# Output projection: its matmuls in four forms, two column blocks each

## The chip, the core and the metric

The kernel runs on one core of a Trainium2 chip. The core has five engines that run side by side: TensorE (PE in the profile; its weight loads are listed apart as PEld), VectorE (DVE), ScalarE (ACT), GpSimd (POOL) and SyncE (SP), whose queue issues the transfers here. TensorE writes its results to PSUM, the other operands lie in SBUF. The metric is the device time of one execution in microseconds (us), from runs of the compiled kernel; lower is better.

## The reference

One layer of a hybrid encoder for 256 tokens with 4096 channels, all float32. The part that the change touches is the projection that brings both branches back into the residual stream:

```python
xn = rms_norm(x, norm_in_g)
proj = xn @ w_in                       # 4096 -> 7 * 2048: q, k, v, z_a, a_c, g_c, z_c
y_a = rms_norm(chunked_attention(q, k, v, rel_table), attn_out_g) * silu(z_a)   # 2048 channels
y_c = rms_norm(conv_module(a_c, g_c, ...), conv_out_g) * silu(z_c)              # 2048 channels
h = x + concatenate([y_a, y_c], axis=-1) @ w_out                                # 4096 x 4096
gate = sigmoid(rms_norm(h, ple_norm_g) @ w_ple_gate + b_ple_gate)
h = h + gate * (p @ w_ple)
return rms_norm(h, final_g)
```

## The kernel before

All large products go through one function, `product`. It makes 512 columns of output for all 256 tokens. Tokens lie on PSUM's partitions, so the two halves of 128 tokens have one accumulator each, `acc[0]` and `acc[1]`, of 128 x 512 float32, which is one PSUM bank. The left operand is kept transposed (channels on partitions) and split into two float32r parts, `xh` and `xl`, whose sum is exact; a `big_t` tile holds four blocks of 128 channels, each with both parts for 256 tokens. The weights are split in the same way: `weight_parts` loads 256 rows by 512 columns (512 KB) on SyncE's queue, ScalarE casts them to the high part `wh` (line 147), VectorE subtracts to get the low part `wl` (line 148). Loaded tiles have five buffers, `wh` and `wl` three each.

`accumulate` adds one block of 128 channels for one half of the tokens in three passes: `xh` times `wh` (line 158), `xh` times `wl` (line 159), `xl` times `wh` (line 160). The activations are the stationary operand, 128 x 128, and the weights move, 512 columns at a time. In `product` the loops are: chunks of two channel blocks, then the block, then the token half, then the three passes. A product over 4096 channels is 16 chunks, or 192 matmuls.

The output projection is a loop over eight blocks of 512 output columns. Each loads its part of `x` (tile `hc`), calls `product` on `w_out`, adds the accumulators to `hc` one token half after the other (line 556, VectorE), sums squares (ScalarE), and transposes the result with eight TensorE transposes of 128 x 128 (line 118) into the operand of the gate product, which is split on ScalarE and VectorE (lines 106 and 107).

No order is written by hand around this loop. The tile framework schedules the instructions and puts in the semaphores; it moves the eight transposes of a block behind the first matmuls of the next one, so that the residual adds have time to finish. Accumulators have four buffers in PSUM, which is two products' worth. After the projection come the embedding products over two channel blocks, whose stationary tile is `pT_in`, and the gate products.

Of the kernel before, what the change touches and what calls it, by code (L numbers as in the profile page):

```python
# [16 lines left out]
P = 128  # L17
NB = 512
# [6 lines left out]
def hybrid_block(  # L25
# [23 lines left out]
    nc = tc.nc  # L49
    _, T, D = x.shape  # L50
    NH = T // P
# [3 lines left out]
    HD = AW // H  # L55
# [3 lines left out]
    KD = D // P  # L59
    KCW = CW // P  # L60
    GH = NB // HD
# [21 lines left out]
    nc.gpsimd.memset(mhalf, -0.5)  # L83

    def rsqrt(dst, src, n):
        """dst = (src / n + eps) ** -0.5, element by element."""
        nc.vector.tensor_scalar(dst, src, 1.0 / n, EPS, ALU.mult, ALU.add)  # L87
        nc.gpsimd.tensor_tensor(dst, dst, mhalf[:, : dst.shape[1]], ALU.pow)  # L88

# [1 line left out]
    gin_rows = cpool.tile([KD, P], F32, name="gin_rows")  # L91
    nc.sync.dma_start(gin_rows, norm_in_g[0].rearrange("(k q) -> k q", q=P))
    gin_ps = tmp_psum()
# [2 lines left out]
    with tc.high_priority():  # L96
        nc.vector.tensor_copy(g_in, gin_ps[:, :KD])

# [1 line left out]
    def big_tile():  # L100
        return big.tile([P, 4, 2, T], F32R, tag="big", name="big_t")

    def split_from_psum(dst, i, src, scale):
        """dst[:, i] = the exact float32r parts of src * scale, a [128, T] block."""
        hi, lo = dst[:, i, 0, :], dst[:, i, 1, :]
        nc.scalar.activation(hi, src, AF.Identity, scale=scale)  # L106
        nc.vector.scalar_tensor_tensor(  # L107
            lo, src, scale, hi.bitcast(F32), ALU.mult, ALU.subtract
        )

    def transposed_split(src, dst, g, col0):
        """src [128, NH, 512] (tokens in rows) to dst's four blocks of [128, T]."""
        for pair in range(2):
            pt = tmp_psum()
            for i in range(2):
                b = 2 * pair + i
                for h in range(NH):
                    nc.tensor.transpose(  # L118
                        pt[:, i * T + h * P : i * T + (h + 1) * P],
                        src[:, h, b * P : (b + 1) * P],  # L120
                        ident,
                    )
            for i in range(2):
                b = 2 * pair + i
                split_from_psum(dst, b, pt[:, i * T : (i + 1) * T], g[:, col0 + b : col0 + b + 1])

# [1 line left out]
    later = deque()  # L128

    def fill(n):  # L130
        for _ in range(min(n, len(later))):
            later.popleft()()

# [1 line left out]
    def weight_parts(w, col, k0, kc, tiles=None):  # L135
        """Rows of kc blocks from block k0: the float32r parts of w, high and low."""
        wt = wpool.tile([P, KC, NB], F32, tag="w", name="wt")
        nc.sync.dma_start(
            wt[:, :kc, :],
            w[k0 * P : (k0 + kc) * P, col : col + NB].rearrange("(k q) n -> q k n", q=P),  # L140
        )
        if tiles is None:
            tiles = [
                wpool.tile([P, KC, NB], F32R, tag=tag, name=tag, bufs=3) for tag in ("wh", "wl")
            ]
        wh, wl = tiles
        nc.scalar.copy(wh[:, :kc, :], wt[:, :kc, :])  # L147
        nc.vector.tensor_tensor(  # L148
            wl[:, :kc, :], wt[:, :kc, :], wh[:, :kc, :].bitcast(F32), ALU.subtract
        )  # L150
        return wh, wl

    def accumulate(acc, h, lhs, kb, wh, wl, k, kblocks):
        t, i = lhs[kb // 4], kb % 4
        xh = t[:, i, 0, h * P : (h + 1) * P]
        xl = t[:, i, 1, h * P : (h + 1) * P]
        first, last = kb == 0, kb == kblocks - 1
        nc.tensor.matmul(acc, xh, wh[:, k, :], start=first, stop=False)  # L158
        nc.tensor.matmul(acc, xh, wl[:, k, :], start=False, stop=False)  # L159
        nc.tensor.matmul(acc, xl, wh[:, k, :], start=False, stop=last)  # L160

    def product(w, col, lhs, kblocks, pool=None, tag="acc", ahead=None, lag=()):
        """[tokens, 512] in PSUM, one tile for each half of the tokens. With lag, pairs of
        tiles that keep the last weights, the second half stops before those and comes with
        a function that adds them."""
        acc = [
            (pool or ps_acc).tile([P, NB], F32, tag=tag, name=f"acc{h}") for h in range(NH)
        ]
        starts = list(range(0, kblocks, KC))
        kept = starts[len(starts) - len(lag) :] if lag else []  # L170
        held = []
        for k0 in starts:
            kc = min(KC, kblocks - k0)
            keep = k0 in kept
            wh, wl = weight_parts(w, col, k0, kc, lag[kept.index(k0)] if keep else None)
            if keep:
                held.append((k0, kc, wh, wl))
            for k in range(kc):
                for h in range(1 if keep else NH):
                    accumulate(acc[h], h, lhs, k0 + k, wh, wl, k, kblocks)  # L180
            if ahead:
                ahead(k0 + kc)
            fill(2)

        def rest():
            for k0, kc, wh, wl in held:
                for k in range(kc):
                    accumulate(acc[1], 1, lhs, k0 + k, wh, wl, k, kblocks)

        return (acc, rest) if lag else acc  # L190
# [8 lines left out]
        rsqrt(r, r, n)  # L199
        return r  # L200

# [1 line left out]
    ssq_x = cpool.tile([P, NH, D // NB], F32, name="ssq_x")  # L203
    xT = []

# [12 lines left out]
        )  # L218

    def load_ahead(kb):  # L220
        """Called after the products of the blocks before kb; the next four are half done."""
        if kb % 4 == 2 and kb // 4 + 1 < D // NB:
            load_x(kb // 4 + 1)

# [35 lines left out]
            dw[:, 4 * c : 4 * c + 4, :], dps[:, : 4 * 32].rearrange("q (i t) -> q i t", t=32)  # L260
        )

# [1 line left out]
    conv = []  # L264

    def conv_tap(cv, uT, i, b, k):
# [38 lines left out]
                later.append(partial(conv_tap, cv, uT, i, 4 * c + i, k))  # L305
        conv.append(cv)

# [1 line left out]
    uS = []  # L309

    def layer_norm_swish():
        """Adds the steps to the work that waits; they leave the split result in uS."""
        add = nc.gpsimd.tensor_tensor
        st = {}

# [10 lines left out]
            nc.scalar.copy(st[key], m)  # L326

        def mean(s):
            """Mean over all channels, on every partition."""
            m = tmp_psum()  # L330
            nc.tensor.matmul(m[:, :T], mean_w, fold(s), start=True, stop=True)
            stat("mu", m[:, :T])
# [18 lines left out]
                add(st["q"], st["q"], s, ALU.add)  # L351

        def variance(s):
            """1 / deviation of each token, tokens on partitions."""
            s = fold(s)
            m = tmp_psum()
            for h in range(NH):
                nc.tensor.matmul(
                    m[:, h : h + 1], s[:, h * P : (h + 1) * P], mean_w[:, :1],
                    start=True, stop=True,  # L360
                )
            st["r"] = cpool.tile([P, NH], F32, name="r_ln")
            rsqrt(st["r"], m[:, :NH], 1)

        def spread(s):
            """The same on every partition, tokens along the free axis."""
            m = tmp_psum()
            for h in range(NH):
                d = s[:, 0, h * P : (h + 1) * P]
# [33 lines left out]
        for c in range(n):  # L403
            later.extend(partial(split, c, i) for i in range(4))

# [1 line left out]
    y_a = []  # L407
    ssq_a = cpool.tile([P, NH, AW // NB], F32, name="ssq_a")

    def to_heads(acc, name):  # L410
        """[tokens, GH * HD] times 1 / rms to [HD, GH, tokens]."""
        st = spool.tile([P, NH, NB], F32, tag="stage", name="st")
        for h in range(NH):
            nc.scalar.activation(st[:, h, :], acc[h], AF.Identity, scale=r_x[:, h : h + 1])
# [83 lines left out]
        heads(g)  # L498
    r_a = rstd_of(ssq_a, AW, "r_a")

# [1 line left out]
    def broadcast_row(src, n0, n):  # L502
        """src[n0 : n0 + n] on every partition."""
        t = spool.tile([P, n], F32, tag="row", name="row")
        nc.sync.dma_start(
            t, bass.AP(tensor=src.tensor, offset=src.offset + n0, ap=[[0, P], [1, n]])
        )
        return t
# [11 lines left out]
        y_c.append(y)  # L520
    r_c = rstd_of(ssq_c, CW, "r_c")

# [1 line left out]
    def gated(y, col, r_y):  # L524
        acc = product(w_in0, col, xT, KD)
        sz = spool.tile([P, NH, NB], F32, tag="stage", name="sz")
# [16 lines left out]
    for c, y in enumerate(y_c):  # L543
        to_operand(y, gc, c)

# [1 line left out]
    hs, hT = [], []  # L547
    ssq_h = cpool.tile([P, NH, D // NB], F32, name="ssq_h")
    for c in range(D // NB):
# [1 line left out]
        nc.sync.dma_start(  # L551
            hc, x[0, :, c * NB : (c + 1) * NB].rearrange("(h q) n -> q h n", q=P)
        )
        acc = product(w_out[0], c * NB, yT, KD)
        for h in range(NH):
            nc.vector.tensor_tensor(hc[:, h, :], acc[h], hc[:, h, :], ALU.add)
            square_sum(ssq_h[:, h, c : c + 1], hc[:, h, :])
# [3 lines left out]
        hT.append(t)  # L561
    r_h = rstd_of(ssq_h, D, "r_h")

# [1 line left out]
    pin = spool.tile([P, NH, PLE], F32, tag="stage", name="pin")  # L565
    nc.sync.dma_start(pin, p[0, 0].rearrange("(h q) n -> q h n", q=P))
    pT = spool.tile([P, PLE // P, 2, T], F32R, tag="hd", name="pT_in", bufs=5)
# [5 lines left out]
            )  # L573
        split_from_psum(pT, b, ppt[:, b * T : (b + 1) * T], 1.0)

# [1 line left out]
    n_f = D // NB  # L577
    ssq_f = cpool.tile([P, NH, n_f], F32, name="ssq_f")

# [75 lines left out]
```

## Time and profile before

| | us |
|---|---|
| median of 3 runs | 2128.86 |
| lowest and highest run | 2128.04, 2129.68 |
| span of the profiled execution, first to last instruction | 2126.7 |
| TensorE busy in it | 2100.4 |
| weight loads busy | 1730.7 |
| VectorE busy | 1268.0 |
| ScalarE busy | 963.2 |

The profile has one execution. Its own time is shown as the span; what lies around the span is in the runs alone. Matmuls overlap in the pipeline: the duration of one is longer than the distance from its start to the next one's start, so the busy times of the three passes add up to more than the span. The output projection runs from about 1384 to 1742 us of the span. In the chain of waits a row gives the start, the length and the work that held the end up; in the timeline a row gives start, length, engine, line and operands, and equal neighbours are merged with their count.

### The profile page before, as it was taken

How to read it: one execution, taken by the hardware profiler on the slowest of the kernel's cores; microseconds unless marked ns; L12 is line 12 of the kernel's file. 1: busy time of each engine (PE TensorE's matmuls, PEld its weight loads, DVE VectorE, ACT ScalarE, POOL GpSimd, SP SyncE). 2: the span in 40 equal slices, each digit the busy share in tenths (PEclk: the TensorE clock that was granted, in tenths of full speed). 3: DMA queues.
4: the chain of work that ended last, by engine and by line, in shares of the span. 5: the costliest groups of instructions: out<-in, count | busy, mean ns of one | idle time of the engine just before them, and what ended most of it. 6: DMA issues, size and time to landing. Idle time of an engine off the chain costs nothing.

```text
span 2126.7 us, 25003 instructions
## 1 busy us (share of the span) xinstructions
PE 2100.4 (99%) x9456; PEld 1730.7 (81%) x9456; DVE 1268.0 (60%) x1609; ACT 963.2 (45%) x1195; POOL 76.3 (4%) x66
## 2 busy tenths in 40 slices
PE   8999999999999999999999999999999999999997
PEld 6788888888888888888888888888888888888886
DVE  5499975498547946765455544464454455455554
ACT  6344445444444444654444444454444454444444
POOL 0000000000000002200000000000000001111110
PEclk9999999999999999999999999999999999999999
DMA  8566665666666665555666666665666656666664
GB/s 273 174 189 192 188 189 177 195 189 187 179 190 188 189 199 167 179 177 198 200 202 203 199 196 191 198 219 188 189 190 192 191 179 206 200 205 201 206 203 173
DMA packets 215065, 412.23 MB, mean 194 GB/s; under 512 B 12948, under 2 KB 15908, under 8 KB 214944
## 3 DMA queue, kind: packets, MB, share of 16 engines
q1 hardware_dynamic: 214944, 410.63, 62.4%
q8 instruction: 74, 1.21, 0.2%
q14 instruction: 47, 0.39, 0.1%
HBM read 406.39 MB, written 4.19 MB: 193 GB/s over the span
## 4 chain that ended last, share of the span: by engine, by line
PE 97%; issue 1%; DMA 1%; DVE 1%; ACT 0%; POOL 0%; SPq 0%; ACTq 0%; POOLq 0%; DVEq 0%
PE acc L158 31%; PE acc L159 31%; PE acc L160 31%; PE tmp_ps L118 1%; PE tmp_ps L421 0%; DMA dwr<-in_w_dw_dram 0%; PE tmp_ps L436 0%; PE tmp_ps L454 0%; DVE cv L343 0%; DMA wt<-in_w_in_dram 0%; DVE wl L148 0%; PE tmp_ps L294 0%; PE tmp_ps L460 0%; PE tmp_ps L461 0%; PE tmp_ps L435 0%
## 5 line engine op out<-in xcount | busy, mean ns | idle before, releaser
L148 DVE TENSOR_TENSOR wl<-wt,wh 128x1024 fp32r<-128x1024 f32 x740 | 919.4, 1244 | 777.4 <-ACT wh L147 776.3
L147 ACT CAST wh<-wt 128x1024 fp32r<-128x1024 f32 x740 | 779.2, 1053 | 1050.5 <-PE acc L160 983.5
L158 PE MATMUL acc<-wh,big_t 128*128 128x512 f32 x2928 | 1146.2, 391 | 5.6 <-ACT big_t L106 5.6
L159 PE MATMUL acc<-wl,big_t 128*128 128x512 f32 x2928 | 1146.6, 392 | 0.6 <-DVE wl L148 0.6
L160 PE MATMUL acc<-wh,big_t 128*128 128x512 f32 x2928 | 1144.1, 391 | 0.0
L158 PEld LDWEIGHTS acc<-wh,big_t 128*128 128x128 f32 x2928 | 550.7, 188 | 119.0 <-ACT big_t L106 6.0
L159 PEld LDWEIGHTS acc<-wl,big_t 128*128 128x128 f32 x2928 | 551.4, 188 | 113.1 <-DVE wl L148 1.3
L160 PEld LDWEIGHTS acc<-wh,big_t 128*128 128x128 f32 x2928 | 551.1, 188 | 113.1
L272 DVE SCALAR_TENSOR_TENSOR cv<-uT,dw,cv 128x256 f32<-128x256 f32 x480 | 201.5, 476 | 0.5
L586 POOL TENSOR_TENSOR hc<-hc,gt 128x512 f32<-128x512 f32 x14 | 24.7, 1784 | 289.8 <-PE acc L160 160.7
L106 ACT ACTIVATE big_t<-tmp_ps,prm 128x256 fp32r<-128x256 f32 x64 | 27.1, 474 | 11.4 <-PE acc L160 5.9
L107 DVE SCALAR_TENSOR_TENSOR big_t<-tmp_ps,prm,big_t 128x256 fp32r<-128x256 f32 x64 | 27.9, 478 | 6.5 <-ACT big_t L106 6.0
L194 ACT ACTIVATE junk<-hc 128x512 bf16<-128x512 f32 x32 | 20.0, 625 | 16.9 <-POOL hc L586 13.9
L88 POOL TENSOR_TENSOR r_h<-r_h,mhalf 128x2 f32<-128x2 f32 x1 | 0.7, 692 | 710.7 <-DVE r_h L87 710.7
L447 ACT ACTIVATE s<-s,nm 128x128 f32<-128x128 f32 (+1 forms) x32 | 14.3, 447 | 9.5 <-DVE nm L446 9.5
L589 POOL TENSOR_TENSOR hc<-hc,row 128x512 f32<-128x512 f32 x14 | 17.8, 1292 | 0.0
L582 DVE SCALAR_TENSOR_TENSOR gt<-acc,r_h,row 128x512 f32<-128x512 f32 x16 | 11.3, 745 | 10.1 <-PE acc L160 10.1
L463 ACT ACTIVATE y_a<-tmp_ps,den 128x128 f32<-128x128 f32 x32 | 10.0, 363 | 14.2 <-PE tmp_ps L461 14.2
L107 DVE SCALAR_TENSOR_TENSOR big_t<-tmp_ps,g_in,big_t 128x256 fp32r<-128x256 f32 x32 | 14.1, 478 | 3.7 <-ACT big_t L106 3.7
L106 ACT ACTIVATE big_t<-tmp_ps,g_in 128x256 fp32r<-128x256 f32 x32 | 13.7, 470 | 5.2 <-DVE big_t L107 3.8
L442 DVE SCALAR_TENSOR_TENSOR s<-tmp_ps,bias 128x128 f32<-128x128 f32 (+1 forms) x32 | 9.9, 352 | 8.9 <-PE tmp_ps L436 8.9
L583 ACT ACTIVATE gt<-gt 128x512 f32<-128x512 f32 x16 | 9.3, 624 | 12.3 <-DVE gt L582 12.3
(136 smaller groups left out, 511.7 us busy)
## 6 DMA issues: line engine op xcount, KB each, us to landing
wt<-in_w_in_dram SPq DMA_DIRECT2D x448, 512.0 KB, 3.7
wt<-in_w_out_dram SPq DMA_DIRECT2D x128, 512.0 KB, 3.5
wt<-in_w_ple_gate_dram SPq DMA_DIRECT2D x128, 512.0 KB, 4.3
wt<-in_w_pw_dram SPq DMA_DIRECT2D x32, 512.0 KB, 3.8
hc<-in_x_dram SPq DMA_DIRECT2D x8, 512.0 KB, 4.2
wt<-in_w_ple_dram SPq DMA_DIRECT2D x8, 512.0 KB, 4.3
out_dram<-hc SPq DMA_DIRECT2D x16, 256.0 KB, 2.8
xin<-in_x_dram SPq DMA_DIRECT2D x7, 512.0 KB, 7.2
```

Source lines behind the costliest of these rows:

```text
L106: nc.scalar.activation(hi, src, AF.Identity, scale=scale)
L107: nc.vector.scalar_tensor_tensor(lo, src, scale, hi.bitcast(F32), ALU.mult, ALU.subtract)
L118: nc.tensor.transpose(pt[:, i * T + h * P : i * T + (h + 1) * P], src[:, h, b * P : (b + 1) * P], ident,)
L147: nc.scalar.copy(wh[:, :kc, :], wt[:, :kc, :])
L148: nc.vector.tensor_tensor(wl[:, :kc, :], wt[:, :kc, :], wh[:, :kc, :].bitcast(F32), ALU.subtract)
L158: nc.tensor.matmul(acc, xh, wh[:, k, :], start=first, stop=False)
L159: nc.tensor.matmul(acc, xh, wl[:, k, :], start=False, stop=False)
L160: nc.tensor.matmul(acc, xl, wh[:, k, :], start=False, stop=last)
L194: nc.scalar.activation(junk, src, AF.Square, accum_out=dst)
L272: nc.vector.scalar_tensor_tensor(cv[:, i, :], uT[:, i, k : k + T], dw[:, b, k : k + 1], cv[:, i, :], ALU.mult, ALU.add,)
L586: (nc.vector if last else nc.gpsimd).tensor_tensor(hc, hc, gt, ALU.add)
L589: nc.gpsimd.tensor_tensor(hc, hc, fg, ALU.mult)
```

## The change

The eight column blocks of the output projection take four forms, two blocks each. Blocks 0 and 1 stay as they were. Blocks 2 and 3 ("turns") put the token halves in turns inside each pass: all three passes alternate between `acc[0]` and `acc[1]`. Blocks 4 and 5 ("narrow") cut every matmul into two of 256 columns, with the same stationary block, one after the other. Blocks 6 and 7 ("moving") exchange the second and third pass, so that `wh` moves twice in a row and `wl` comes last. Every product is the same sum of the same three terms; all other products of the kernel keep the old form.

```diff
+    def parts(h, lhs, kb):
+        t, i = lhs[kb // 4], kb % 4
+        return tuple(t[:, i, j, h * P : (h + 1) * P] for j in range(2))
+
     def accumulate(acc, h, lhs, kb, wh, wl, k, kblocks):
-        t, i = lhs[kb // 4], kb % 4
-        xh = t[:, i, 0, h * P : (h + 1) * P]
-        xl = t[:, i, 1, h * P : (h + 1) * P]
+        xh, xl = parts(h, lhs, kb)
...
+    def accumulate_turns(acc, lhs, kb, wh, wl, k, kblocks):
+        first, last = kb == 0, kb == kblocks - 1
+        for j, (part, w) in enumerate(((0, wh), (0, wl), (1, wh))):
+            for h in range(NH):
+                nc.tensor.matmul(
+                    acc[h], parts(h, lhs, kb)[part], w[:, k, :],
+                    start=first and j == 0, stop=last and j == 2,
+                )
+
+    def accumulate_narrow(acc, h, lhs, kb, wh, wl, k, kblocks):
+        xh, xl = parts(h, lhs, kb)
+        first, last = kb == 0, kb == kblocks - 1
+        for j, (xp, w) in enumerate(((xh, wh), (xh, wl), (xl, wh))):
+            for n in range(2):
+                cols = slice(n * NB // 2, (n + 1) * NB // 2)
+                nc.tensor.matmul(
+                    acc[:, cols], xp, w[:, k, cols],
+                    start=first and j == 0 and n == 0, stop=last and j == 2,
+                    skip_group_check=True,
+                )
+
+    def accumulate_moving(acc, h, lhs, kb, wh, wl, k, kblocks):
+        xh, xl = parts(h, lhs, kb)
+        first, last = kb == 0, kb == kblocks - 1
+        nc.tensor.matmul(acc, xh, wh[:, k, :], start=first, stop=False)
+        nc.tensor.matmul(acc, xl, wh[:, k, :], start=False, stop=False)
+        nc.tensor.matmul(acc, xh, wl[:, k, :], start=False, stop=last)
...
-    def product(w, col, lhs, kblocks, pool=None, tag="acc", ahead=None, lag=()):
+    def product(w, col, lhs, kblocks, pool=None, tag="acc", ahead=None, lag=(), form=None):
...
             for k in range(kc):
+                if form == "turns":
+                    accumulate_turns(acc, lhs, k0 + k, wh, wl, k, kblocks)
+                    continue
+                one = {"narrow": accumulate_narrow, "moving": accumulate_moving}.get(form, accumulate)
                 for h in range(1 if keep else NH):
-                    accumulate(acc[h], h, lhs, k0 + k, wh, wl, k, kblocks)
+                    one(acc[h], h, lhs, k0 + k, wh, wl, k, kblocks)
...
-        acc = product(w_out[0], c * NB, yT, KD)
+        acc = product(
+            w_out[0], c * NB, yT, KD, form=(None, "turns", "narrow", "moving")[c // 2]
+        )
```

The rest of the difference only removes comments and docstrings, so line numbers move.

## The prediction

> **What bounds the kernel.** I read the page first: shares of the span, clock, chain, costliest groups.
>
> ```profile
> span 2126.7 us, 25003 instructions
> PE 2100.4 (99%) x9456; PEld 1730.7 (81%) x9456; DVE 1268.0 (60%) x1609; ACT 963.2 (45%) x1195; POOL 76.3 (4%) x66
> PEclk9999999999999999999999999999999999999999
> PE 97%; issue 1%; DMA 1%; DVE 1%; ACT 0%; POOL 0%; SPq 0%; ACTq 0%; POOLq 0%; DVEq 0%
> PE acc L158 31%; PE acc L159 31%; PE acc L160 31%; PE tmp_ps L118 1%; PE tmp_ps L421 0%; DMA dwr<-in_w_dw_dram 0%; PE tmp_ps L436 0%; PE tmp_ps L454 0%; DVE cv L343 0%; DMA wt<-in_w_in_dram 0%; DVE wl L148 0%; PE tmp_ps L294 0%; PE tmp_ps L460 0%; PE tmp_ps L461 0%; PE tmp_ps L435 0%
> L158 PE MATMUL acc<-wh,big_t 128*128 128x512 f32 x2928 | 1146.2, 391 | 5.6 <-ACT big_t L106 5.6
> L159 PE MATMUL acc<-wl,big_t 128*128 128x512 f32 x2928 | 1146.6, 392 | 0.6 <-DVE wl L148 0.6
> L158 PEld LDWEIGHTS acc<-wh,big_t 128*128 128x128 f32 x2928 | 550.7, 188 | 119.0 <-ACT big_t L106 6.0
> L159 PEld LDWEIGHTS acc<-wl,big_t 128*128 128x128 f32 x2928 | 551.4, 188 | 113.1 <-DVE wl L148 1.3
> ```
>
> TensorE is busy throughout, at over nine tenths of its clock, and 93% of the chain is the three passes of the big products. L158 and L159 use the same stationary block one after the other, yet each has its 2928 weight loads: every matmul brings its own load, repeated operand or not.
>
> The changed stage is the output projection, about 1384 to 1742 us. Next come its busy times (us, then engines with counts, clock, DMA share, GB/s) and its longest waits.
>
> ```profile
> 1384.00:1742.00 358.00, 358.00 (x1618) 295.65 (x1617) 184.58 (x188) 159.71 (x200) 0.00 (x0) 1.00 0.61 193
> ```
>
> ```profile
> ACT wh L147 <- PE acc L160: 179.5, 108, 1.7
> DVE wl L148 <- ACT wh L147: 167.4, 124, 2.5
> PEld tmp_ps L118 <- DVE hc L556: 1.8, 7, 0.3
> ```
>
> ScalarE's casts wait for TensorE to give weight buffers back, VectorE waits for ScalarE; DMA is at 61%. Nothing feeds TensorE late but the residual add, ahead of the transposes at seven block ends. So the price of the change is read from how far apart successive matmuls start. The chain of waits gives those distances (start, length, what):
>
> ```profile
> 1480.01 0.23 PE acc L158
> 1480.24 0.23 PE acc L159
> 1480.46 0.23 PE acc L160
> 1480.69 0.23 PE acc L158
> ...
> 1481.37 0.23 PE acc L158
> ```
>
> Six steps in 1.36 us: 226.7 ns for 512 columns. The 391 ns of the page overlap; they are no step.
>
> **The change, part by part.** The stage has eight blocks of 192 matmuls. Blocks 0 and 1 keep the old form: nothing.
>
> *Blocks 2 and 3, token halves in turns: 0.* The same 384 matmuls and loads in another order. Its typical step (same weight tile, other stationary block, other PSUM tile) is there already: the pass at L160 for one token half is followed by L158 for the other, and in the rows above L160 to L158 takes 0.23 like the others. I take 226.7 ns. The ends: 233.3 ns, the slowest steady step in the trace, below (+6.6 x 384 = +2.5 us), and a step without any fixed part, worked out next (-5.5 us).
>
> *Blocks 6 and 7, passes in another order: 0.* The low weight part is needed one matmul later; each buffer's last reader stays among the chunk's last two matmuls. A cast (ACT) and a subtraction (DVE) lie between the buffer's return and TensorE, of 1.05 and 1.24 us:
>
> ```profile
> L148 DVE TENSOR_TENSOR wl<-wt,wh 128x1024 fp32r<-128x1024 f32 x740 | 919.4, 1244 | 777.4 <-ACT wh L147 776.3
> L147 ACT CAST wh<-wt 128x1024 fp32r<-128x1024 f32 x740 | 779.2, 1053 | 1050.5 <-PE acc L160 983.5
> ```
>
> With three buffers, two further chunks of 12 x 226.7 ns = 2.72 us cover these 2.3 us twice; without that cover each of the 64 chunks of the four reordered blocks would stall by up to 2.3 us. The same two ends as above.
>
> *Blocks 4 and 5, 256 columns: +5.5 us.* 384 matmuls of 512 columns become 768 of 256, with 768 loads. The question is the step of a half-width one; no float32r matmul of 256 columns is in the trace. Two kinds of rows bound it. First the plain float32 ones (chain, then timeline and durations, ns min/median/max):
>
> ```profile
> 950.79 0.22 PE tmp_ps L459 x2
> ...
> 951.46 0.22 PE tmp_ps L435 x2
> 951.68 0.43 PE tmp_ps L436 x2
> ```
>
> ```profile
> 951.51 0.60 PE L436 MATMUL tmp_ps<-kT,qT 128*128 128x256 f32 x2
> ```
>
> ```profile
> L436 PE MATMUL tmp_ps<-kT,qT x32: 379/380/382, 337.0 to 951.7; 128*128 128x256 f32 x32
> ```
>
> 128 columns take 111 ns (950.79 to 951.68, eight steps in 0.89 us); 256 take 215 (0.43 for two) to 220 (0.60 for two less the 0.38 of one), say 217.5. So 128 columns more cost 106 ns, and 5 ns are a fixed part that every matmul pays. A float32r column costs at most 226.7 / 512 = 0.44 ns against 0.83 here. Taken as half of 0.83 (an estimate from these rows), 512 columns are 212.5 ns and the fixed part of a float32r step is 14.2 ns. That some part is fixed the other rows show, in the embedding products, with the same 512 columns and another stationary tile (chain of waits):
>
> ```profile
> 1788.63 0.23 PE acc L158
> 1788.86 0.24 PE acc L159
> ...
> 1790.03 0.23 PE acc L158
> ```
>
> Six steps in 1.40 us, 233.3 ns: 6.6 ns change with the load alone. So a half-width step is 106.2 + 14.2 = 120.4 ns, a pair 240.9 against 226.7, and 384 x 14.2 = 5.5 us.
>
> The lower end is the floor that a load sets. Transposes of 128 columns, each with its load, and two float32r loads behind them (timeline; then one transpose's duration):
>
> ```profile
> 1430.16 0.82 PE L118 MATMUL tmp_ps<-ident,hc 128*128 128x128 f32 x6
> ```
>
> ```profile
> 1430.70 0.19 PEld L159 LDWEIGHTS acc<-wl,big_t 128*128 128x128 f32 x1
> 1430.81 0.19 PEld L160 LDWEIGHTS acc<-wh,big_t 128*128 128x128 f32 x1
> ```
>
> ```profile
> L118 PE MATMUL tmp_ps<-ident,hc x62: 270/273/325, 1429.4 to 1741.9; 128*128 128x128 f32 x62
> ```
>
> (0.82 - 0.27) / 5 = 0.11 us a transpose, and 0.11 us from load to load: a pair is not under 220 ns, -6.7 x 384 = -2.6 us. The upper end has the fixed part of the embedding products, 233.3 - 212.5 = 20.8 ns, on each half: 254 ns a pair, +10.5 us. I stay with +5.5, since these blocks read the same kind of stationary tile as the 226.7 ns rows.
>
> The Trainium skill, TensorE: Matmul & The Clock Gate, section Back-to-back issue gap, gives a warm step as columns / 2.4 + 2.5 ns: 216 ns for 512, 109 for 256. By that rule a pair would be 218 and the two blocks 3 us cheaper. Here the rows disagree for 512 already, 226.7 against 216, so I go by the rows.
>
> *Block ends: +1.0 us.* One end as it is (timeline; the last row begins the next one):
>
> ```profile
> 1428.68 1.28 DVE L556 TENSOR_TENSOR hc<-acc,hc 128x512 f32<-128x512 f32 x2
> 1428.74 0.39 PE L160 MATMUL acc<-wh,big_t 128*128 128x512 f32 x1
> 1428.97 0.39 PE L158 MATMUL acc<-wh,big_t 128*128 128x512 f32 x1
> 1429.42 0.43 PE L118 MATMUL tmp_ps<-ident,hc 128*128 128x128 f32 x2
> ...
> 1473.90 0.32 PE L118 MATMUL tmp_ps<-ident,hc 128*128 128x128 f32 x1
> ```
>
> The next block starts at 1428.97; after two of its matmuls TensorE reaches two transposes, which need the first token half's add, and later six that need the second's. The first takes effect 0.05 us late (0.43 for the two instead of 0.27 + 0.11), so it is ready 1429.42 + 0.05 - 1428.97 = 0.50 us after the block's start. The first half's last matmul began three steps before 1428.74. In the instruction order of the changed program:
> - After blocks 2 and 3 both halves end with the last two matmuls, so the first add is 2 x 0.227 = 0.45 us later and the transposes are ready at 0.95. They stand after three whole matmuls (0.68) and six narrow ones (0.72): waits of 0.27 and 0.23, less the 0.05 of today, +0.40.
> - After block 4 they stand after two narrow matmuls (0.24), after block 5 after one whole (0.23); readiness by the same steps is 0.46: +0.17 and +0.18.
> - After block 7, one matmul instead of two ahead of them: 0.50 - 0.23 - 0.05 = +0.22. After block 6 they come 48 matmuls late instead of 40: 0.
>
> Together 0.97 us; between 0, if other waits take these in, and 1.5, if the six transposes are late too. TensorE never idles otherwise, so nothing gives this back.
>
> *The sum.* 5.5 + 1.0 = +6.5 us on the profiled span of 2126.7, so 2133.2. The median of the runs, 2128.86, lies 2.2 us over the span: 2135.4 us.
>
> **Rivals.**
> 1. *The half step follows the columns or the load's floor*, 110 to 113 ns. For: loads 0.11 us apart, transposes at 0.11. Against: 5 ns fixed in float32, 6.6 ns that turn on the load. Halves of 113.3 cost 0, of 110 -2.6 us; with the block ends -1.6 to +1.0, about 2129. The step of the skill's page above would end here too.
> 2. *The load isn't hidden behind a half-width matmul.* A load lasts 188 ns and there is one for each half. At 188 ns a step, a pair is 376: +149 x 384 = +57 us, 2187. Against: starts 0.11 us apart say that loads overlap each other; for: a transpose's load is no float32r load, and only two of the latter are seen so close. The Trainium skill, Perfetto Trace Analysis, Identifying the Most-Contended Engine, judges TensorE by the share of LDWEIGHTS time; by it a narrow block, with 384 loads of 0.188 us = 72 us, could not fit into its 43.5 us, and this same time would follow.
> 3. *The reordered blocks step like the embedding products*, 233.3 ns, since what follows what around a load has changed: 768 x 6.6 = +5.1 on top, 2140.5. For: such steps exist; against: they come with another stationary tile.
> 4. *Faster: the fixed part is a stall between two matmuls that add into the same PSUM addresses.* Turns change the bank at each step and the narrow form the column half; both lose 14.2 ns. Turns: -5.5. Narrow: the load's floor, -2.6. With +1.0 for block ends: -7.1, 2121.8. It decides once more than 5.3 us (the 4.3 of the bound and the block ends) is gained. Against: the L160 to L158 step changes banks today and is no shorter.
>
> That the change does nothing because repeated stationary blocks share a load is ruled out by the equal counts of L158 and L159.
>
> **How the numbers follow.** Chances: forecast 0.60, rival 1 0.26, rival 2 0.06, rival 3 0.05, rival 4 0.03. The runs lie within 0.08%; 0.2%, 4.3 us, is about what tells a change from none, so slower begins at 2133.1. The forecast's own range goes from a fixed part of 8 ns (+3.1, block ends 0.5) to 20.8 ns and 1.5: 2132.4 to 2140.9; a tenth of its chance lies under 2133.1. Slower: 0.54 + 0.06 + 0.05 = 0.65. Same: 0.06 + 0.26 = 0.32. Faster: 0.03. The range, 2128.5 to 2141.0, holds the forecast, rival 3 and over half of rival 1, about 0.8.
>
> **What would show it.** In the profile after, the two narrow blocks last about 47.2 us each instead of 44.5 (1429.42 to 1473.90 between first transposes today), their 768 matmuls start 120 ns apart, and weight loads are busy nearly all the time there. The four reordered blocks keep 226.7 ns. The add ahead of the transposes releases TensorE for about 3 us in all instead of 1.8. The prediction is wrong if half steps are at 113 or less, if they are at 140 or more, or if turns move off 226.7.

## The result and the profile after

The changed kernel takes 2133.27 us (median of 13 runs, 2132.01 to 2134.24), the kernel before 2128.86 (13 runs, 2127.51 to 2130.13): 4.4 us more, a ratio of 1.002 with a 95% interval of 1.0012 to 1.0028. The forecast was 2135.4 us and "slower". The measured change lies just above the prediction's own bound of 0.2% (4.3 us), and its interval begins below it.

The profiled execution spans 2132.5 us, 5.8 more than the one before; it is the longest of its 13 runs (2134.24 us with what lies around). From its page: span, shares, and the groups of the narrow (L181), turned (L169) and exchanged (L193) forms.

```profile
span 2132.5 us, 25780 instructions
PE 2106.0 (99%) x9840; PEld 1752.5 (82%) x9840; DVE 1268.6 (59%) x1609; ACT 961.8 (45%) x1195; POOL 76.3 (4%) x66
L181 PE MATMUL acc<-wh,big_t 128*128 128x256 f32 x512 | 83.0, 284 | 0.0
L181 PEld LDWEIGHTS acc<-wh,big_t 128*128 128x128 f32 x512 | 70.9, 192 | 0.1
L169 PE MATMUL acc<-wl,big_t 128*128 128x512 f32 x128 | 39.8, 391 | 0.0
L193 PE MATMUL acc<-wl,big_t 128*128 128x512 f32 x128 | 49.9, 390 | 0.0
```

384 more matmuls and 384 more loads, and TensorE's busy time has grown by 5.6 us. The chain of waits after, in the turned, the narrow and the exchanged blocks (start, length, what; equal neighbours are merged):

```profile
1534.98 2.04 PE acc L169 x9
```

```profile
1579.98 2.04 PE acc L181 x17
```

```profile
1689.94 0.23 PE acc L192
1690.17 0.23 PE acc L193
1690.40 0.23 PE acc L191
...
1691.98 0.23 PE acc L192
```

Nine turned steps in 2.04 us are 226.7 ns, nine exchanged ones from 1689.94 to 1691.98 are 226.7 ns, both as before. Seventeen narrow ones in 2.04 us are 120.0 ns. So a pair of halves costs 240.0 where a whole matmul costs 226.7, and 768 x 0.1200 - 384 x 0.2267 = 5.1 us. That is the change.

The rest of the span's difference is not in it: the first residual transpose, which ends block 0 in the old form, starts at 1430.06 instead of 1429.42, so 0.6 us were lost earlier, in code that is the same. Busy times of two stretches, one inside each narrow block, show what the loads do there (columns as in the prediction):

```profile
1563.90:1610.40 46.50, 46.50 (x390) 46.47 (x388) 22.47 (x23) 18.94 (x25) 0.00 (x0) 1.00 0.61 182
1610.50:1657.40 46.90, 46.90 (x392) 46.80 (x391) 20.73 (x18) 17.87 (x20) 0.00 (x0) 1.00 0.59 180
```

Weight loads are busy all the time there, and a load's record is 192 ns, but a matmul starts every 120 ns: the loads overlap.

### The profile page after: what moved, and what is told of

Same layout as the page of the kernel before. It is cut to its first block, busy times and chain, and to the rows that moved or that the text cites. A ratio compares the mean times of both kernels' runs of the same rounds, so it can differ in the third digit from the quotient of the medians.

```text
span 2132.5 us, 25780 instructions
## 1 busy us (share of the span) xinstructions
PE 2106.0 (99%) x9840; PEld 1752.5 (82%) x9840; DVE 1268.6 (59%) x1609; ACT 961.8 (45%) x1195; POOL 76.3 (4%) x66
## 4 chain that ended last, share of the span: by engine, by line
PE 97%; issue 1%; DMA 1%; DVE 1%; ACT 0%; POOL 0%; SPq 0%; ACTq 0%; POOLq 0%; DVEq 0%
PE acc L160 27%; PE acc L161 27%; PE acc L162 27%; PE acc L181 4%; PE acc L169 4%; PE acc L192 1%; PE acc L193 1%; PE acc L191 1%; PE tmp_ps L118 1%; PE tmp_ps L458 0%; PE tmp_ps L473 0%; DMA dwr<-in_w_dw_dram 0%; PE tmp_ps L491 0%; DMA wt<-in_w_in_dram 0%; DVE cv L380 0%
## 5 line engine op out<-in xcount | busy, mean ns | idle before, releaser
L160 PE MATMUL acc<-wh,big_t 128*128 128x512 f32 x2544 | 997.4, 392 | 5.6 <-ACT big_t L106 5.6
L161 PE MATMUL acc<-wl,big_t 128*128 128x512 f32 x2544 | 997.7, 392 | 0.6 <-DVE wl L148 0.6
L162 PE MATMUL acc<-wh,big_t 128*128 128x512 f32 x2544 | 995.4, 391 | 0.0
L160 PEld LDWEIGHTS acc<-wh,big_t 128*128 128x128 f32 x2544 | 479.1, 188 | 104.0 <-ACT big_t L106 6.0
L161 PEld LDWEIGHTS acc<-wl,big_t 128*128 128x128 f32 x2544 | 479.6, 189 | 98.4 <-DVE wl L148 1.2
L162 PEld LDWEIGHTS acc<-wh,big_t 128*128 128x128 f32 x2544 | 479.3, 188 | 98.1
L181 PE MATMUL acc<-wh,big_t 128*128 128x256 f32 x512 | 83.0, 284 | 0.0
L181 PEld LDWEIGHTS acc<-wh,big_t 128*128 128x128 f32 x512 | 70.9, 192 | 0.1
L169 PE MATMUL acc<-wh,big_t 128*128 128x512 f32 x256 | 69.0, 390 | 0.0
L169 PEld LDWEIGHTS acc<-wh,big_t 128*128 128x128 f32 x256 | 47.9, 188 | 9.8
L181 PE MATMUL acc<-wl,big_t 128*128 128x256 f32 x256 | 52.0, 284 | 0.0
L191 PE MATMUL acc<-wh,big_t 128*128 128x512 f32 x128 | 50.0, 391 | 0.0
L192 PE MATMUL acc<-wh,big_t 128*128 128x512 f32 x128 | 49.9, 390 | 0.0
L193 PE MATMUL acc<-wl,big_t 128*128 128x512 f32 x128 | 49.9, 390 | 0.0
L181 PEld LDWEIGHTS acc<-wl,big_t 128*128 128x128 f32 x256 | 40.0, 192 | 0.0
L169 PE MATMUL acc<-wl,big_t 128*128 128x512 f32 x128 | 39.8, 391 | 0.0
```

What stands on the lines that cost most here:

```text
L169: nc.tensor.matmul(acc[h], parts(h, lhs, kb)[part], w[:, k, :], start=first and j == 0, stop=last and j == 2,)
L181: nc.tensor.matmul(acc[:, cols], xp, w[:, k, cols], start=first and j == 0 and n == 0, stop=last and j == 2, skip_group_check=True,)
L192: nc.tensor.matmul(acc, xl, wh[:, k, :], start=False, stop=False)
L193: nc.tensor.matmul(acc, xh, wl[:, k, :], start=False, stop=last)
```

## The experiments

Theory A: a float32r matmul costs its columns, 106.7 ns per 256, and a fixed 13.3 ns more; 226.7 and 120.0 fit that, but two points fit any line. Rivals: the 120 is the load's own pace; the fixed part is a stall between neighbours (same PSUM addresses, another stationary block); it is the load's reading; or the 4.4 us have little to do with the narrow form. In the runs "before" is the old kernel on the same chip. `form` is the list of forms by block in the diffs; blocks that aren't named keep the old form.

**All eight blocks in one form.**

```diff
-            w_out[0], c * NB, yT, KD, form=(None, "turns", "narrow", "moving")[c // 2]
+            w_out[0], c * NB, yT, KD, form="turns"        # and "moving", and "narrow"
```

> All eight blocks of the output projection in turns, nothing narrow. Theory A (a float32r matmul costs its columns, 106.7 ns per 256, plus a fixed 13.3 ns, whatever stands next to it: 226.7 and 120.0 ns in the changed kernel): every step stays at 226.7 ns, the time at 2128.9 us give or take 1 for the block ends. Rival (order matters: turns change the accumulator at each step and gain or lose by it): 1536 steps move by some ns each, 1.5 us for each ns.

> All eight blocks with the second and third pass exchanged, nothing narrow. Theory A: steps stay at 226.7 ns, 2128.9 us give or take 1. Rival (the order of passes matters, since the low weights come last or one weight tile moves twice in a row): 1536 steps move, 1.5 us for each ns.

> All eight blocks with 256 columns a matmul. Theory A: 1536 pairs of 240.0 instead of 226.7 ns, +20.5 us, 2149.3 us. Rival (the 4.4 us of the change lie at the block ends or in the reordered blocks, and the narrow blocks have only a part): 4.4 us would not grow to 20; with half of it from narrow blocks, +9 us.

Turns: 2129.46 us against 2128.56, ratio 1.0004 (0.9995 to 1.0013). Exchanged passes: 2129.41, ratio 1.0002 (0.9993 to 1.0011). Narrow: 2149.5, ratio 1.0098 (1.0081 to 1.0115), +20.9 us where 20.5 were expected (brackets hold 95% intervals). The chain of waits in the three, about 1580 us:

```profile
1579.81 2.27 PE acc L169 x10
```

```profile
1579.85 0.23 PE acc L192
...
1581.89 0.23 PE acc L192
```

```profile
1579.94 2.16 PE acc L181 x18
```

227, 226.7 (nine steps in 2.04 us) and 120.0 ns. Four times as many narrow blocks cost four times as much (20.9 us against 5.1), and order alone costs nothing that these runs can tell.

**Neighbours: columns outside, passes inside** (blocks 4 and 5).

```diff
-        for j, (xp, w) in enumerate(((xh, wh), (xh, wl), (xl, wh))):
-            for n in range(2):
-                cols = slice(n * NB // 2, (n + 1) * NB // 2)
+        for n, cols in enumerate((slice(0, 256), slice(256, NB))):
+            for j, (xp, w) in enumerate(((xh, wh), (xh, wl), (xl, wh))):
```

> Blocks 4 and 5 in halves of 256 columns, but the three passes of the first column half come before those of the second, so that neighbours have another stationary block in two of three steps and add into the same PSUM addresses; the other blocks in the old form. Theory A: 120.0 ns a step, +5.1 us. Rival (the fixed part is a stall of matmuls that add into the same addresses, or repeating the stationary block in the narrow form saved something): the step differs from 120 by 5 ns or more, 768 of them, 3.8 us.

2133.59 us against 2128.56, +5.0. The chain:

```profile
1579.96 2.04 PE acc L200 x17
```

Again 120.0 ns. Which stationary block and which PSUM addresses the matmul before used makes no difference here: the fixed part is no stall of neighbours.

**The load's floor: uneven halves and quarters** (blocks 4 and 5).

```diff
-            for n in range(2):
-                cols = slice(n * NB // 2, (n + 1) * NB // 2)
+            for n, cols in enumerate([slice(0, 320), slice(320, NB)]):
+            # quarters: for n, cols in enumerate([slice(i, i + 128) for i in range(0, NB, 128)]):
```

> Blocks 4 and 5 cut into 320 and 192 columns instead of halves, the others in the old form. Theory A with a floor of 110 to 112 ns set by the next load: from the 320 to the 192 start 133.3 + 13.3 = 146.7 ns; from the 192 to the 320 the floor, since 80 + 13.3 = 93.3 is under it; a pair of 257 to 259 ns, +12 us. Rival B (120 ns of the narrow form is itself the load's pace, no fixed part): 146.7 or less, and 120; a pair of up to 267 ns, +15 us. Rival C (no floor by loads down to 93 ns): a pair of 240 ns, +5.1 us.

> Blocks 4 and 5 in quarters of 128 columns, the others in the old form. Theory A with the load's floor: 110 to 112 ns a step, 384 groups of four of 440 to 448 instead of 226.7 ns, +82 to +85 us. Rival B (the load's pace is 120): 480 ns, +97 us. Rival C (no floor): 53.3 + 13.3 = 66.7 ns a step, 267 ns, +15.4 us.

Uneven: 2142.49 us against 2128.33, +14.2, ratio 1.0063 (1.0041 to 1.0086). Quarters: 2212.88, +84.6, ratio 1.0392 (1.0362 to 1.0422). The chains:

```profile
1579.96 2.07 PE acc L200 x16
```

```profile
1579.93 2.12 PE acc L200 x19
```

Sixteen uneven steps in 2.07 us are 258.8 ns a pair; nineteen quarters in 2.12 us are 111.6 ns each. The quarters decide: a pace of 120 (rival B: 480 for four, +97 us) and no floor (rival C: 267, +15.4 us) are both out, and there is a floor of 112 ns. The uneven run rules out rival C alone (a pair of 240); its interval, +9 to +18 us, holds both +12 and rival B's +15, and a pair of 258.8 is within B's "up to 267".

The pair has the length of 146.7 + 112, but the matmuls don't start in that rhythm. In the uneven run's timeline, matmuls and then loads:

```profile
1579.80 0.25 PE L200 MATMUL acc<-wl,big_t 128*128 128x192 f32 x1
1579.88 0.69 PE L200 MATMUL acc<-wh,big_t 128*128 128x320 f32 x4
```

```profile
1580.32 0.30 PEld L200 LDWEIGHTS acc<-wl,big_t 128*128 128x128 f32 x2
1580.58 0.56 PEld L200 LDWEIGHTS acc<-wh,big_t 128*128 128x128 f32 x4
```

From a 192 to the next 320 it is 0.08 us; the medians over the run are 171 ns from a 320 to a 192 and 88 back. It is the loads that come near the two numbers, with 150 and 108 ns in turn (medians), and none of them starts less than 108 ns after another. So the floor of 108 to 112 ns belongs to the loads, and matmuls can start closer together than that. Halves of 256 columns lie 8 ns over it, so their 120.0 is columns and fixed part.

**What the fixed part belongs to: half a load, and bfloat16** (blocks 4 and 5).

```diff
+        m = slice(0, P if first else P // 2)
...
-                nc.tensor.matmul(acc, xp, w[:, k, :], ...)
+                nc.tensor.matmul(acc[m, :], xp[:, m], w[:, k, :], ...)
```

```diff
+        xb = yb[:, kb % 3, h * P : (h + 1) * P]          # bfloat16, from the first tile of yT
...
-                nc.tensor.matmul(acc[:, cols], xp, w[:, k, cols], ...)
+                nc.tensor.matmul(acc[:, cols], xb, w.bitcast(BF16)[:, k, cols], ...)
```

> Blocks 4 and 5 with stationary blocks of 64 columns instead of 128 after the first channel block, still 512 moving columns: a load of half the length for each matmul. It leaves out the second 64 tokens of each half in those blocks, from the second channel block on. Theory A (the fixed part belongs to the matmul): 226.7 ns a step, 0 us. Rival D (the fixed part is the load's reading in the way of the moving operand, in proportion to its length): 220 ns, -2.5 us.

> Blocks 4 and 5 with bfloat16 operands, 512 columns: weights cast to a high and a low bfloat16 part, and one bfloat16 tile of activations used for all channel blocks, so these two blocks don't compute the projection. Theory A1 (the fixed 13.3 ns belongs to operands of 4 bytes at this rate): the step falls to between 213.3 and the 218 that the plain float32 matmul's fixed 5 ns would give, -3.3 to -5.1 us. Theory A2 (it belongs to any pair of load and matmul): 226.7 ns, 0 us.

> As with the wide bfloat16 blocks, in halves of 256 columns; blocks 4 and 5 don't compute the projection. Theory A1 (the 13.3 ns belongs to 4-byte operands): the step is 106.7 plus 0 to 5 ns, or the load's floor if bfloat16 loads have the same, 109 to 112 ns, a pair of 218 to 224 ns, -3.3 to -1.0 us. Theory A2 (any pair of load and matmul): 120 ns, +5.1 us.

Half a load: 2129.84 us against 2128.33, ratio 1.0005 (0.9993 to 1.0016). bfloat16: 2124.63 wide, ratio 0.9982 (0.9970 to 0.9993), and 2126.10 narrow against 2128.34, ratio 0.9990 (0.9979 to 1.0002). The chains of the three, and the load of 64 columns from the groups by form:

```profile
1579.79 3.21 PE acc L200 x14
```

```profile
L200 PEld LDWEIGHTS acc<-wh,big_t 128*64 128x64 f32 x242 | 32.5, 134 | 22.9
```

```profile
1579.97 2.16 PE acc L208 x10
```

```profile
1579.90 2.18 PE acc L208 x20
```

A load of 64 columns lasts 134 ns instead of 188, but the step is 229.3 ns: 2.6 longer, not 6.7 shorter. Rival D falls, and that the step grew was in nobody's expectation. With bfloat16 operands the steps are 216 and 109 ns: 2.7 and 2.3 over 213.3 and 106.7, and the fixed part of 13.3 ns is nearly gone. It goes with the float32r operands, theory A1. The Trainium skill, TensorE: Matmul & The Clock Gate, section Back-to-back issue gap, gives columns / 2.4 + 2.5 ns as the warm gap of a single matmul, which is 216 and 109 ns here; for a sustained stream of loads and matmuls it gives about 131 ns at 512 columns. The trace agrees with the first figure for bfloat16 and not for float32r, and no run here shows a step near 131 ns at 512 columns. Whether the stationary or the moving float32r operand brings the 13.3 ns, these runs don't tell: both changed together, and with them the record of a load, 98 ns in bfloat16 instead of 188.

**The 233.3 ns of the embedding products.** The prediction used them as its upper end. Their stationary tile lay 32 bytes off a multiple of 64 in each partition, the stationary tiles of the other big products and the weights lay on one. (The buffers that it shares are 4576 bytes each, 71.5 times 64, so every second one begins 32 bytes off.)

```diff
-        uT = spool.tile([P, 4, PAD + T], F32, tag="hd", name="uT", bufs=5)
+        uT = spool.tile([P, 4, PAD + T + 2], F32, tag="hd", name="uT", bufs=5)
```

> All eight blocks in the old form; one tile of the convolution, which sets the size of a rotating buffer, grows from 4576 to 4608 bytes per partition, so that the embedding products' stationary tile begins at a multiple of 64 bytes, where it began 32 bytes off. Theory E (the 233.3 ns of these products come from where the stationary tile lies): their 96 steps fall to 226.7, -0.6 us in all, to be read from the steps alone. Rival F (they come from what goes before, a short product after a wait): 233.3 stays.

2127.02 us against 2128.34, ratio 0.9992 (0.9981 to 1.0004): no difference that the runs can tell. The chain in the embedding products:

```profile
1788.57 0.23 PE acc L160
...
1789.93 0.23 PE acc L160
```

Six steps in 1.36 us are 226.7 ns, down from 233.3. So where the tile lies is what made the 233.3 of these 96 matmuls. The next two runs give the same offset to all the big products, once for the stationary and once for the moving operand. The diff is that of the first; in the second, the two pads stand around `wpool`.

```diff
+    pad_a = ctx.enter_context(tc.tile_pool(name="pad_a", bufs=1))
+    pad_a.tile([P, 8], F32, name="pad_a_t")               # 32 bytes per partition
     big = ctx.enter_context(tc.tile_pool(name="big", bufs=12))
+    pad_b = ctx.enter_context(tc.tile_pool(name="pad_b", bufs=1))
+    pad_b.tile([P, 8], F32, name="pad_b_t")
     wpool = ctx.enter_context(tc.tile_pool(name="wpool", bufs=5))
```

> Old form throughout; 32 bytes of padding ahead of the tiles that hold the big products' stationary operands (and again behind them, so that the moving weights stay where they were), which puts the stationary tiles 32 bytes off a multiple of 64. Theory E (a stationary tile 32 bytes off costs what the embedding products showed, 233.3 instead of 226.7 ns): 8784 steps dearer by 6.6 ns, +58 us. Rival F (the embedding products owed their 233.3 to something else that the larger buffer changed too): 226.7 ns, 0 us.

> Old form throughout; the same 32 bytes of padding around the weight tiles instead, so that the moving operand is 32 bytes off and the stationary one isn't. Theory E (it is the load that suffers): 226.7 ns, 0 us. Rival G (any operand that isn't at a multiple of 64 bytes adds a read to each matmul): steps dearer by some ns, 8.8 us for each ns.

2179.71 and 2180.76 us against 2129.20, ratios 1.0239 (1.0210 to 1.0269) and 1.0244 (1.0214 to 1.0274). The chains, stationary tiles off, then weights off:

```profile
1479.88 0.23 PE acc L164
1480.11 0.23 PE acc L165
...
1481.98 0.23 PE acc L164
```

```profile
1479.97 0.23 PE acc L164
1480.20 0.23 PE acc L165
...
1481.37 0.23 PE acc L164
```

Nine steps in 2.10 us and six in 1.40: 233.3 ns in both. So it isn't the load that suffers, as Theory E had it: moving either operand by 32 bytes costs the same 6.6 ns. 8784 of them make 58 us; 51 were measured. In the traces the mean distance to the next start, waits included, grew from 229.6 to 235.5 and 235.6 ns, 52 us; distances over 250 ns became fewer (164 before, 142 and 143 here), so waits took in a part.

Both traces also hold a few matmuls with both operands 32 bytes off. With the stationary tiles off, these are 48 at the end, whose weights are kept in the same pool as the stationary tiles. With the weights off, they are the embedding products, whose tile is 32 off as before. The timelines:

```profile
2146.96 0.39 PE L165 MATMUL acc<-big_t 128*128 128x512 f32 x1
...
2148.32 0.39 PE L165 MATMUL acc<-big_t 128*128 128x512 f32 x1
```

```profile
1879.42 0.40 PE L164 MATMUL acc<-wh,pT_in 128*128 128x512 f32 x1
...
1882.22 0.40 PE L164 MATMUL acc<-wh,big_t 128*128 128x512 f32 x1
```

Six steps in 1.36 us are 226.7 ns; twelve in 2.80 are 233.3. So being off a multiple of 64 isn't dear by itself (rival G as it was put), nor is having both operands off always free. One reading fits all these cases: the step is 226.7 where the starts of the two operands lie a multiple of 128 bytes apart, and 233.3 where they don't. By the pools' sizes the distance modulo 128 is 0 in all the fast products, 32 or 96 in the slow ones with one operand off, and 64 in the embedding products of the last run, where the pads moved the weights by 32 bytes and the embedding tile by 64. No run was made to test this reading, so it stays a conjecture.

## Why the prediction was right, and where it was off

*Turns and exchanged passes, 0.* Right: 226.7 ns in both forms, and the medians of whole kernels of either are within 0.1% of the old one. The step from L160 to L158, taken from the trace of before, was the right row. Rival 3 (233.3 ns in the reordered blocks) falls with these steps; the 233.3 on which it rested has its cause in where a tile starts in memory.

*Narrow, +5.5 us.* Right in mechanism, +5.1 in size. The term that was off by a little is the fixed part, 14.2 ns by the float32 rows against 13.3 measured; it came from rows rounded to 0.01 us. One of the two supports for a fixed part was misread: "6.6 ns change with the load alone" is wrong, since the 6.6 ns come and go with where a tile lies, and moving the weights by 32 bytes brings them as well. They say nothing of the load, neither against rival 1 nor as the upper end of 254 ns a pair. What carried the forecast is the float32 rows alone. The choice between fixed part and load's floor, on which the forecast hung, came out as argued, though the quarters show that the floor, 111.6 ns, is only 8 ns away. Rival 1 would have needed that floor to bind. Rival 2 falls: the share of load time is full (46.47 of 46.50 us) and the step is 120 ns all the same, since loads overlap. The share of LDWEIGHTS time, by which the Trainium skill, Perfetto Trace Analysis, section Identifying the Most-Contended Engine, judges TensorE, read full here without setting the step. Rival 4 falls with the turned blocks, which kept 226.7 ns, and with the columns outside.

*Block ends, +1.0 us.* Wrong: about 0. From the first transposes after block 0 to those after block 7 it is 311.44 us before (1429.42 to 1740.86) and 316.49 after (1430.06 to 1746.55): 5.05 more, which is the narrow term alone. The waits of the transposes for the residual add, over the stage, after:

```profile
PEld tmp_ps L118 <- DVE hc L595: 1.5, 6, 0.3
```

1.5 us in 6 waits, not the 3 that were forecast, and less than the 1.8 of before. The step of this term that failed is "the first add is 0.45 us later" after the turned blocks. It took the add to start as soon as its matmul was done. VectorE's timeline before, just ahead of the add at 1428.68, and then the timeline at the end of block 2 after:

```profile
1427.53 1.23 DVE L148 TENSOR_TENSOR wl<-wt,wh 128x1024 fp32r<-128x1024 f32 x1 [1.50 <-ACT wh L147]
```

```profile
1518.16 1.07 PE L169 MATMUL acc<-wh,big_t 128*128 128x512 f32 x4
1518.58 1.29 DVE L595 TENSOR_TENSOR hc<-acc,hc 128x512 f32<-128x512 f32 x2 [0.19 <-PE acc L169]
1519.06 0.39 PE L169 MATMUL acc<-wl,big_t 128*128 128x512 f32 x1
1519.33 0.44 PE L118 MATMUL tmp_ps<-ident,hc 128*128 128x128 f32 x2
```

Before, VectorE was in a weight subtraction until 1428.76, so the add was held by that and not by TensorE. After, VectorE is free and waits 0.19 us for TensorE. The new block starts two steps after 1518.16, at 1518.61: the add is 0.03 us ahead of it where it was 0.29 ahead, 0.26 later and not 0.45. The transposes then run at 1519.33 and are 0.06 late, 0.78 after the block's start instead of the forecast 0.95, so their wait is 0.10 and not 0.27. At the other ends the waits of before and after differ by tenths both ways and cancel.

*The sum.* +6.5 forecast, +4.4 measured, with an interval of +2.6 to +6.0. The narrow term alone, 5.1, lies in it. That the change came out over the prediction's bound of 4.3 us and not under it was close, and in part luck.

## What to carry to other kernels

Where TensorE is the bound and every matmul brings its own weight load, the price of a form is read from the distance between the starts of successive matmuls, not from their durations: here a float32r matmul costs its columns (106.7 ns per 256) plus 13.3 ns, with a floor of 112 ns for the loads. So halving the columns costs 6%, and quartering them nearly doubles the time of the block, while the orders of passes, token halves and PSUM banks cost nothing that the runs can tell. Before a wait is moved, look what its engine was doing while it waited: the add that looked late for its matmul was queued behind a subtraction. Watch where the stationary and the moving float32r tile start in memory: moving one of them by 32 bytes against the other cost 51 us of 2129 here. With both at a multiple of 64 bytes the steps of 128 x 512 were at 226.7 ns in every run; what the exact rule is, these runs don't settle.

## What was not expected of the hardware

- The fixed part goes with the operands' type: 13.3 ns with float32r (226.7 and 120.0 ns for 512 and 256 columns), 2.3 to 2.7 with bfloat16 (216 and 109).
- One operand's tile moved by 32 bytes against the other's costs 6.6 ns a matmul, 233.3 instead of 226.7, whichever of the two it is. With both moved it was 226.7 ns in 48 matmuls and 233.3 in 96 others.
- Float32r loads start no closer than 108 ns (uneven) and 110 ns (quarters) after one another, while a matmul of 320 columns starts 88 ns (median) after the one of 192 before it.
- A load of half the length (134 instead of 188 ns) made the step longer, 229.3 ns; why stays open.
